# Two gate rows from matmuls of the spread products with ones, in a gMLP/S5 and PEER layer

## The chip, the core and the metric

The kernel runs on one core of a Trainium2 chip. The core has TensorE (PE, matmuls, with PEld for its weight loads), VectorE (DVE), ScalarE (ACT), GpSimd (POOL) and SyncE (SP, which issues transfers). The metric is the device time of one execution in microseconds (us), lower is better.

## The reference

One decoder layer on x of 1024 tokens x 1024, float32, with a conditioning vector c of 1024:

```python
mod = silu(c) @ w_ada + b_ada                      # 6 x 1024
sh1, sc1, gt1, sh2, sc2, gt2 = split(mod, 6)
h = rmsnorm(x, g_mix) * (1 + sc1) + sh1
z = h @ w_in                                       # u, v halves of a gMLP (512 each), S5 input (512)
y = concat(sgu(zu, zv), s5(zs)) @ w_out
x = x + gt1 * y
h2 = rmsnorm(x, g_ffn) * (1 + sc2) + sh2
x = x + gt2 * peer(h2)                             # 8 heads, product keys, top 16 of 16384 experts
return rmsnorm(x, g_final)
```

`gt1` and `gt2` are the gates: rows of 1024 numbers, the same for each token.

## The kernel before

The tokens are eight blocks of 128. The four blocks of a half share the input projection (`pzs` for the S5 input, `pzv` and `pzu` for the gMLP), and the S5 part is done for both halves at once: local convolutions and transfers of states as matmuls (`py` from `U`, `TOE` and from the scanned states `X` with `CN`), with the scan over chunks on VectorE in between (`t_s`, `X`, `fx`). The result `Yg` goes to DRAM (`ys_d`) and comes back transposed (`ysT`). Then come the GLU (`pg` matmuls with `wg`, sigmoid `sg`, product `ss`), the gMLP's mixing (`pmx`, `mx`, `gm`, from the normed `vn`), the output projection of a block (`po`, from `gm` and `ss` with `wo`), its gate and residual (`outproj`, L643 and L644: `po` times `bc`, plus `x`), the norm (`xn`), its transpose (`ptf`, `tq`), the PEER query (`pq`, with `wq`) and scores (`psc`, `sc`), and the routing on VectorE (`scr`, `m`, `ixs`). Blocks 0 to 4 go through a dense path: their gates are put into a table over all experts (`put`: `a`, `b`, `pgs`, `GS`), and from about 885 us on TensorE goes through 128 tiles of experts (`stage1`: `pa`; `stage2`: `res`, `pd`). Blocks 5 to 7 gather their experts' rows by indirect transfers on GpSimd beside that.

Each `mod[i]` is a column tile, 128 x 8. Its sums run on VectorE: eight chunks of `w_ada` (`wada`), each times its column of `cs` (the silu of c), are added into a spread tile of 128 x 1024 (`mp` in PSUM for i = 2 and 4, copied to `mc`; `mc` itself for i = 5, in `mod5`), so that what is left is the sum over the 128 partitions. `mod_late` does that sum with eight matmuls of 128x1 against a column of ones (`pm`) and adds the bias column. i = 2 is the first gate, i = 5 the second.

Where a gate is needed as a row over all partitions, `row_bcast` makes it from the column: for each of eight pieces VectorE writes a diagonal tile (`diag`), and a matmul of ones with it fills 128 columns of `pb`; ScalarE copies the 1024 columns to SBUF (`bc`). The first row (`gate1`, item `g1`) is used by all `outproj`. The second (`late_gt2`, item `gt`) is stored to DRAM (`gt2_d`) for the end of the kernel.

The tiles `mc`, `x`, `xn`, `mx`, `sg`, `bc2` share three slots (tag `x`); `mp`, `pb` and `po` share PSUM's tag `b`. Up to 885 us the code is written as generators, and an order of their steps is worked out from a table by hand (`plan`: start and duration of each item) and from each item's needs (`items`). A list scheduler then sets every engine's final order from that program and its own estimates; each engine takes its instructions strictly in that order.

Of the kernel before, what the change touches and what calls it, by code (L numbers as in the profile page):

```python
# [8 lines left out]
F32 = mybir.dt.float32  # L9
# [7 lines left out]
ALU = mybir.AluOpType  # L17
# [4 lines left out]
P = 128  # L22
S = 1024
D = 1024
KD = D // P
# [18 lines left out]
    op0=(-238.2, 44.5), sb0=(-21, 248.8), m5=(-490.1, 3.4), r0=(234.1, 82.1), op1=(132.1, 27.3), op2=(292.7, 7.7),  # L44
# [1 line left out]
    r2=(434.5, 89.3), s1=(746.9, 213.2), zu=(417.8, 124.5), sb3=(451.1, 27.3), r3=(536.2, 48.7),  # L46
    s2=(469.7, 305.5), gl=(553.5, 5.5), op4=(543.1, 6.2), op5=(577.6, 1.8), sb4=(663, 101), r4=(445.7, 88.9),
    s3=(833.5, 73.1), op6=(590.2, 7.7), sb5=(768.6, 1.7), op7=(897.9, 60.4), sb6=(809.8, 27.4), sb7=(892.4, 30.9),
    gt=(858.2, 122), rel=(739, 334), s4=(981.8, 131.5), r5=(916.4, 58.6), r6=(989.9, 124.6), ld=(776, 675.7),
    oa0=(-275.5, 62.3), oa1=(155.8, 9.5), oa2=(314.1, 7), oa3=(240.1, 5.1), oa4=(394.7, 40.1), oa5=(594, 15.7),  # L50
    oa6=(572.9, 5.5), oa7=(898.3, 28.1), z0=(-1650.9, 29.9), f1=(-1496.2, 24.1), z1=(-1253, 33.5),
    pa=(-1479.5, 58), pb=(-1364.9, 1.6), pc=(-1507.3, 44.1), cs=(-1171.2, 4.5), lu=(-1201.3, 17.4),
    k0=(-1496.6, 7.4), sn=(-1527.9, 6.3), m2=(-1355.9, 33), m4=(-1275.1, 28.3), pw=(-1348.9, 7.4),
    si=(-1231.9, 3.7), k1=(-1347, 1.5), av=(-1141.5, 2.5), wu=(-1185.4, 101), cst=(-1132.1, 14.6),
    sc=(-1112.1, 4.9), wq0=(-1115, 14.4), wq1=(-1142.8, 77.1), au=(-1181.6, 1.4), wo0=(-1165.4, 1),
    wo1=(-962.7, 7.3), so=(-926.7, 23.4), vn=(-891, 2.4), g1=(-703.9, 14.2), ax=(-882.1, 8.1), m3=(-856.1, 38.5),
    ag=(-741.7, 2.7), mid=(-803.3, 8.8), wo2=(-878.1, 13.4), wo3=(-805.6, 6.4), wq2=(-441.9, 1.1),
    wq3=(-808.5, 91.5), ky=(-851.1, 72.1)))

# [38 lines left out]
def tile_hybrid_layer(ctx: ExitStack, tc: tile.TileContext, a, out, cfg=CFG):  # L98
    nc = tc.nc
    V, A, G, T = nc.vector, nc.scalar, nc.gpsimd, nc.tensor  # L100
    NGB = cfg["ngb"]
    NDB = NB - NGB
# [23 lines left out]
    def bankB(name):  # L126
        return psB.tile([P, 2, 512], F32, tag="b", name=name)
# [81 lines left out]
    early = {}  # L209

    def mod_sums(i):
        mp = bankB(f"mp{i}").rearrange("p a b -> p (a b)")
        k = 0
        for w, n in early[i]:
            for kk in range(n):
                if k:
                    V.scalar_tensor_tensor(mp, w[:, kk], cs[:, k:k + 1], mp, op0=ALU.mult, op1=ALU.add)
                else:
                    V.tensor_scalar(mp, w[:, kk], cs[:, k:k + 1], None, op0=ALU.mult)
                k += 1  # L220
            yield
        mc = sm.tile([P, D], F32, tag="x", name=f"mc{i}", bufs=3)
        A.copy(mc, mp)
        mod_late(i, mc)

    def mod_load(i, src):
        ws, k = [], 0
        for c in src:
            n = {"X": 4, "p": 2, "x": 1}[c]
            v = a["w_ada"][k * P:(k + n) * P, i * D:(i + 1) * D].rearrange("(k p) n -> p k n", p=P)  # L230
            if c == "X":
                w = sB.tile([P, 4, D], F32, tag="X", name=f"wada{i}_{k}", bufs=1)
# [280 lines left out]
    wzu = []  # L513
# [16 lines left out]
    def z_u(hf, wz):  # L530
        y = slotA([P, 4, HT], f"gm{hf}")
        gm.append(y)
        for n in range(4):
            pz = bankA(f"pzu{hf}_{n}")
            for k in range(KD):
                T.matmul(pz, wz(k)[:, n * P:(n + 1) * P], hT[hf][k // 4][:, k % 4, :], start=(k == 0), stop=(k == KD - 1))
            A.activation(y[:, n, :], pz, AF.Gelu_apprx_tanh)
            yield
# [10 lines left out]
            if j % 2:  # L549
                yield  # L550

    def row_bcast(dst, col, name):
        pb = bankB(f"pb_{name}")
        for k in range(KD):
            dg = sm.tile([P, P], F32, tag="diag", name=f"diag_{name}{k}", bufs=2)
            V.tensor_scalar(dg, ident, col[:, k:k + 1], None, op0=ALU.mult)
            T.matmul(pb[:, k // 4, (k % 4) * P:(k % 4 + 1) * P], ones, dg, start=True, stop=True)
        A.copy(dst, pb.rearrange("p a b -> p (a b)"))
        return dst

# [36 lines left out]
    def load_wo(i, slot):  # L597
        wo[i] = slot([P, 2, D], f"wo{i}")
        nc.sync.dma_start(wo[i], a["w_out"][i * 256:(i + 1) * 256, :].rearrange("(k p) n -> p k n", p=P))

    def gate1():
        nonlocal gt1
        gt1 = row_bcast(sm.tile([P, D], F32, name="bc1", bufs=1), mod[2], "gt1")
        yield

    def glu(hf, slot):
        wg = slot([P, 4, 512], f"wg{hf}")
# [22 lines left out]
    def outproj(b):  # L630
# [19 lines left out]
                xns[b] = sm.tile([P, D], F32, tag="x", name=f"xn{b}", bufs=3)  # L650
                V.tensor_scalar(xns[b], x1, r2[:, b:b + 1], None, op0=ALU.mult)
        yield

    def late_gt2():
        bc2 = sm.tile([P, D], F32, tag="x", name="bc2", bufs=3)
        nc.scalar.dma_start(gt2_d, row_bcast(bc2, mod[5], "gt2"))

    gx = kp = sC = tk = iot = iot8 = None

# [386 lines left out]
    def lead(i0, i1):  # L1046
        for i in range(i0, i1):
            yield from stage1(i)

    def mod5():  # L1050
        mc = sm.tile([P, D], F32, tag="x", name="mc5", bufs=3)
        for k in range(0, KD, 2):
            w = slotC([P, 2, D], f"wada5_{k}")
            nc.sync.dma_start(w, a["w_ada"][k * P:(k + 2) * P, 5 * D:].rearrange("(k p) n -> p k n", p=P))
            for kk in range(2):
                if k + kk:
                    V.scalar_tensor_tensor(mc, w[:, kk], cs[:, k + kk:k + kk + 1], mc, op0=ALU.mult, op1=ALU.add)
                else:
                    V.tensor_scalar(mc, w[:, kk], cs[:, 0:1], None, op0=ALU.mult)
            if k == KD - 2:  # L1060
                mod_late(5, mc)
            yield

    def gt2_row():
        late_gt2()
        yield

    def mod4():
        yield from mod_sums(4)
# [2 lines left out]
    def prep_steps(n):  # L1072
# [10 lines left out]
        si=(s5_in, 4, "sn lu"), sc=(scan, 1, "si pw cs"), so=(s5_out, 8, "sc k1"),  # L1083
        av=(lambda: z_v(0, slotA([P, 4, 512], "vn0"), wzv), 4, "z0"), vn=(lambda: v_norm(0), 4, "av sc cst"),
        cst=(lambda: one(load_cst), 1, "z0"), wu=(lambda: one(load_wzu), 1, "z0"),
        au=(lambda: z_u(0, wzu[0]), 4, "wu"), ax=(lambda: mix(0), 2, "au vn"), g1=(gate1, 1, "m2"),
        ag=(lambda: glu(0, slotA), 4, "so"), mid=(mid, 1, "so m2 m4 m3"), m5=(mod5, 4, "mid sc"),
        ky=(lambda: one(lambda: nc.scalar.dma_start(keys, a["peer_keys"])), 1, "z0"),
        zv=(half1_v, 4, "mid vn z1"), zu=(half1_u, 6, "zv op1 op2 op3"), gl=(lambda: glu(1, slotS), 4, "ag"),
        gt=(gt2_row, 1, "m5"), rel=(release, NDB, "gt op7 sb7"), ld=(lambda: lead(0, L), 2 * L, "rel"))  # L1090
    for i in range(4):
        items[f"wq{i}"] = lambda i=i: one(load_wq, i), 1, f"wq{i - 1}" if i else "z0"
        items[f"wo{i}"] = lambda i=i: one(load_wo, i, slotC if i // 2 else slotS), 1, "mid" if i // 2 else "z0"
    for b in range(NB):
# [398 lines left out]
```

## Time and profile before

| | |
|---|---|
| runs | 2655.66, 2656.88, 2659.79 us; median 2656.88 |
| the profiled execution | 2655.86 us, span 2653.9 us |
| TensorE busy | 2538.1 us, 96% of the span |
| VectorE busy | 2267.8 us, 85% |
| ScalarE busy | 1312.8 us, 49% |
| GpSimd busy | 1180.9 us, 44% |
| transfers | 726.85 MB, 274 GB/s over the span |

A busy time is the time in which an engine executes; a busy engine isn't always the one that the end depends on. A matmul of float32 data leaves two records in the trace, so a "x16" of matmuls is eight instructions. The granted clock (PEclk) is 1.00 for 2.4 GHz and 0.50 for 1.2 GHz.

### The profile page before, as it was taken

To read this page: it belongs to the slowest core of one execution; us is meant where nothing else is said; L and a number is where in the kernel's file an instruction comes from. 1 tells how busy PE (TensorE), PEld (TensorE's weight loads), DVE (VectorE), ACT (ScalarE), POOL (GpSimd) and SP (SyncE) were. 2 spreads that over 40 slices of the span, in tenths; PEclk is the share of its full clock that TensorE was granted. 3 is DMA by queue.
4 is the path that set the end of the run, shared out by engine and by line. 5 is a ranking of instruction groups with operands and counts; after the bars stand their busy time and mean duration, and the time that the engine had idled before them with its cause. 6 is when DMAs were issued, how large, how long until landed. Compare 5 with 4: busy or idle time off the path is not lost. (4 is left out here: it accounts for less than half of the span.)

```text
span 2653.9 us, 39049 instructions
## 1 busy us (share of the span) xinstructions
PE 2538.1 (96%) x14119; PEld 2168.1 (82%) x14119; DVE 2267.8 (85%) x4215; ACT 1312.8 (49%) x2315; POOL 1180.9 (44%) x842
## 2 busy tenths in 40 slices
PE   6999999999877999999999999999999999999997
PEld 2548677678666898989999989999999988999986
DVE  7984699869899888789989888889999888899898
ACT  2311246568868377773222577762223767732222
POOL 0001000000000177676667578766665767776660
PEclk9996999999988999999999999999999999999999
DMA  9546233444636699999999999899998999999993
GB/s 362 108 121 217 101 122 104 126 136 135 181 118 193 218 328 326 343 327 364 341 340 375 325 336 330 331 354 364 341 355 326 334 345 343 325 368 345 343 365 139
DMA packets 301761, 726.85 MB, mean 274 GB/s; under 512 B 42448, under 2 KB 133072, under 8 KB 301152
## 3 DMA queue, kind: packets, MB, share of 16 engines
q0 software_dynamic: 112832, 411.09, 42.4%
q1 hardware_dynamic: 165600, 254.48, 28.6%
q10 hardware_dynamic: 23136, 58.79, 6.2%
q8 instruction: 111, 1.82, 0.3%
q14 instruction: 82, 0.67, 0.1%
HBM read 660.70 MB, written 62.39 MB: 272 GB/s over the span
## 5 line engine op out<-in xcount | busy, mean ns | idle before, releaser
L888 POOL DMA_INDIRECT ru<-in_peer_u_dram,ix x384 | 637.7, 1661 | 897.6 <-issue 745.1
L959 PE MATMUL pa<-Th,u 128*128 128x320 f32 x4096 | 911.3, 310 | 4.9 <-DVE u L936 3.1
L959 PEld LDWEIGHTS pa<-Th,u 128*128 128x128 f32 x4096 | 688.4, 188 | 8.7 <-DVE u L936 3.6
L888 POOL DMA_INDIRECT rv<-in_peer_v_dram,ix x384 | 522.8, 1361 | 257.4 <-DVE gacc L916 168.0
L959 PE MATMUL pa<-Tl,u 128*128 128x320 f32 x2048 | 633.4, 309 | 0.0
L899 DVE TENSOR_TENSOR ru<-ru,hn 128x2048 f32<-128x2048 f32 x192 | 438.6, 2289 | 113.1 <-DMA ru<-in_peer_u_dram,ix 106.6
L894 ACT ACTIVATE jk<-ru 128x1024 bf16<-128x1024 f32 x384 | 405.4, 1056 | 213.2 <-issue 167.7
L916 DVE SCALAR_TENSOR_TENSOR gacc<-rv,act,gacc 128x1024 f32<-128x1024 f32 x381 | 489.2, 1284 | 6.4 <-DVE u L936 0.4
L1006 PE MATMUL pd<-v,wh 128*128 128x512 f32 x1280 | 402.6, 390 | 3.2 <-ACT wh L980 1.6
L997 PE MATMUL res<-v,wh 128*128 128x512 f32 x1280 | 400.7, 390 | 0.8 <-ACT wh L980 0.8
L959 PEld LDWEIGHTS pa<-Tl,u 128*128 128x128 f32 x2048 | 385.3, 188 | 1.7
L1006 PEld LDWEIGHTS pd<-v,wh 128*128 128x128 f32 x1280 | 238.8, 188 | 52.5 <-ACT wh L980 2.5
L997 PEld LDWEIGHTS res<-v,wh 128*128 128x128 f32 x1280 | 239.6, 188 | 50.4 <-ACT wh L980 1.6
L961 ACT ACTIVATE w<-pa 128x320 f32<-128x320 f32 x256 | 108.7, 431 | 333.7 <-PE pa L959 311.9
L698 ACT ACTIVATE b<-hot,gT 128x128 f32<-128x128 f16 x520 | 233.5, 537 | 61.0 <-PE pgs L700 36.0
L1006 PE MATMUL pd<-v,wl 128*128 128x512 f32 x640 | 248.7, 390 | 1.7 <-DVE wl L982 1.6
L997 PE MATMUL res<-v,wl 128*128 128x512 f32 x640 | 248.1, 389 | 1.3 <-DVE wl L982 1.3
L935 ACT CAST u<-ur 128x1024 fp32r<-128x1024 f32 x128 | 133.5, 1043 | 205.3 <-DMA ur<-in_peer_ut_dram 79.0
L700 PE MATMUL pgs<-a,b 128*128 128x128 f32 x1280 | 188.9, 299 | 46.2 <-DVE a L690 19.3
L700 PEld LDWEIGHTS pgs<-a,b 128*128 128x128 f32 x1280 | 169.9, 207 | 68.4 <-ACT b L698 35.3
L936 DVE TENSOR_TENSOR u<-ur,u 128x1024 fp32r<-128x1024 f32 x128 | 156.3, 1221 | 29.7 <-ACT u L935 23.2
L943 ACT CAST v<-vr 128x1024 fp32r<-128x1024 f32 x128 | 133.7, 1045 | 94.1 <-DMA vr<-in_peer_v_dram 76.8
(349 smaller groups left out, 3050.4 us busy)
## 6 DMA issues: line engine op xcount, KB each, us to landing
vr<-in_peer_v_dram SPq DMA_DIRECT2D x128, 512.0 KB
ur<-in_peer_ut_dram SPq DMA_DIRECT2D x128, 512.0 KB
G_d<-GS SPq DMA_DIRECT2D x40, 1024.0 KB
Gt<-G_d ACTq DMA_DIRECT2D x64, 640.0 KB
wada<-in_w_ada_dram SPq DMA_DIRECT2D x17, 1024.0 KB
wo<-in_w_out_dram SPq DMA_DIRECT2D x8, 1024.0 KB
ru<-in_peer_u_dram,ix POOLq DMA_INDIRECT x384
rv<-in_peer_v_dram,ix POOLq DMA_INDIRECT x384
```

The lines of the kernel that those rows point to most:

```text
L698: A.activation(b1[:, n], hot[:, :, o + n], AF.Copy, scale=gT[:, s1 + o + n:s1 + o + n + 1])
L700: T.matmul(pg[:, o // 4, (o % 4) * P:(o % 4 + 1) * P], b1[:, o % 2], a1[:, o % 4], start=True, stop=True)
L888: G.indirect_dma_start(out=row[:, e], out_offset=None, in_=a[src], in_offset=bass.IndirectOffsetOnAxis(ap=ix[:, s0 + e:s0 + e + 1], axis=0))
L894: A.activation(junk, row[:, e], AF.Copy, accum_out=act[:, s + e:s + e + 1])
L899: V.tensor_mul(row, row, bcast(hn, 1, GP))
L916: V.scalar_tensor_tensor(ac, row[:, e], w, ac, op0=ALU.mult, op1=ALU.add)
L935: A.copy(u[:, 0], ur)
L936: V.tensor_tensor(u[:, 1], ur, u[:, 0].bitcast(F32), op=ALU.subtract)
L943: A.copy(v[:, 0], vr)
L959: T.matmul(pa[:, :NN], l[:, k, :], r[:, k, ns], start=(k == 0 and m == 0), stop=(k == KD - 1 and m == 2))
L997: T.matmul(res[tb][n], l[:, ts], r[:, n * 512:(n + 1) * 512], start=(g == 0 and q == 0 and m == 0), stop=(g == NGR - 1 and q == QG - 1 and ...
L1006: T.matmul(po, l[:, ts], r[:, n * 512:(n + 1) * 512], start=(q == 0 and m == 0), stop=(q == QG - 1 and m == 2))
```

## The change

`row_bcast` goes. A new function `gate_row` loads the gate's bias as one row (`br`, on one partition), and sums the spread products `mc` over the partitions with a whole matrix of ones as the stationary operand, so that each partition of `pb` gets the complete row; a second matmul over one partition adds the bias row. The first row is made at the end of `mod_sums(2)`, in place of `mod_late`; the second at the end of `mod5`, with its store. The items `g1` and `gt` go, and what needed them needs `m2` and `m5`.

```diff
@@ plan
-    gt=(858.2, 122), rel=(739, 334), s4=(981.8, 131.5), r5=(916.4, 58.6), r6=(989.9, 124.6), ld=(776, 675.7),
+    rel=(739, 334), s4=(981.8, 131.5), r5=(916.4, 58.6), r6=(989.9, 124.6), ld=(776, 675.7),
...
-    wo1=(-962.7, 7.3), so=(-926.7, 23.4), vn=(-891, 2.4), g1=(-703.9, 14.2), ax=(-882.1, 8.1), m3=(-856.1, 38.5),
+    wo1=(-962.7, 7.3), so=(-926.7, 23.4), vn=(-891, 2.4), ax=(-882.1, 8.1), m3=(-856.1, 38.5),
@@ mod_sums
         mc = sm.tile([P, D], F32, tag="x", name=f"mc{i}", bufs=3)
         A.copy(mc, mp)
-        mod_late(i, mc)
+        if i == 2:
+            gt1 = sm.tile([P, D], F32, name="bc1", bufs=1)
+            gate_row(i, mc, gt1)
+        else:
+            mod_late(i, mc)
@@ new
+    def gate_row(i, mc, dst):
+        br = sm.tile([P, D], F32, tag="x", name=f"br{i}", bufs=3)
+        nc.sync.dma_start(br[:1].rearrange("o (k p) -> o k p", p=P), a["b_ada"][:, i * KD:(i + 1) * KD].rearrange("p (o k) -> o k p", o=1))
+        pb = bankB(f"pb{i}")
+        for n in range(2):
+            for r, p in ((mc, P), (br, 1)):
+                T.matmul(pb[:, n], ones[:p], r[:p, n * 512:(n + 1) * 512], start=(p == P), stop=(p == 1))
+        A.copy(dst, pb.rearrange("p a b -> p (a b)"))
@@ gone
-    def row_bcast(dst, col, name):
-        pb = bankB(f"pb_{name}")
-        for k in range(KD):
-            dg = sm.tile([P, P], F32, tag="diag", name=f"diag_{name}{k}", bufs=2)
-            V.tensor_scalar(dg, ident, col[:, k:k + 1], None, op0=ALU.mult)
-            T.matmul(pb[:, k // 4, (k % 4) * P:(k % 4 + 1) * P], ones, dg, start=True, stop=True)
-        A.copy(dst, pb.rearrange("p a b -> p (a b)"))
-        return dst
...
-    def gate1():
-        nonlocal gt1
-        gt1 = row_bcast(sm.tile([P, D], F32, name="bc1", bufs=1), mod[2], "gt1")
-        yield
...
-    def late_gt2():
-        bc2 = sm.tile([P, D], F32, tag="x", name="bc2", bufs=3)
-        nc.scalar.dma_start(gt2_d, row_bcast(bc2, mod[5], "gt2"))
@@ mod5
             if k == KD - 2:
-                mod_late(5, mc)
-            yield
-
-    def gt2_row():
-        late_gt2()
-        yield
+                bc2 = sm.tile([P, D], F32, tag="x", name="bc2", bufs=3)
+                gate_row(5, mc, bc2)
+                nc.scalar.dma_start(gt2_d, bc2)
+            yield
```

In DRAM `b_ada` lies as 128 x 48, so that the 1024 numbers of a row `br` are 4-byte elements 192 bytes apart.

The program shows where the instructions now stand. On TensorE, between the last `pzv` (the v projection) and the first `py`, before:

```order
L491 MATMUL pzv_3_1100<-wzv_306,hT_1_130 128x512 x4
L248 MATMUL pm_1113<-ones,mc_1111 128x1 x8
L536 MATMUL pzu_0_1464<-hT_0_129,wzu_1123 128x512 x4
L536 MATMUL pzu_0_1464<-hT_1_130,wzu_1124 128x512 x4
L536 MATMUL pzu_1_1474<-hT_0_129,wzu_1123 128x512 x4
```

and of the change:

```order
L505 MATMUL pzv_3_1100<-wzv_305,hT_0_129 128x512 x4
L505 MATMUL pzv_3_1100<-wzv_306,hT_1_130 128x512 x4
L256 MATMUL pb_1116<-mc_1111,ones 128x512
L256 MATMUL pb_1116<-br_1114,ones 128x512
L256 MATMUL pb_1116<-mc_1111,ones 128x512
L256 MATMUL pb_1116<-br_1114,ones 128x512
L550 MATMUL pzu_0_1463<-hT_0_129,wzu_1122 128x512 x4
```

Eight matmuls of one column each have become four of 512 columns, ahead of the u projection (`pzu`) and all that follows. On TensorE between the last `pg` of the first half and the first `pq`, before (`pm_1900` is the column of row 5, `po_1916` and `po_2043` are blocks 0 and 1):

```order
L617 MATMUL pg_3_1848<-ysT_1818,wg_1816 128x512 x2
L637 MATMUL po_1916<-wo_1506,gm_1463 128x512
L557 MATMUL pb_gt_1857<-diag_gt_1873,ones 128x128
L557 MATMUL pb_gt_1857<-diag_gt_1876,ones 128x128
L637 MATMUL po_1916<-wo_1506,gm_1463 128x512
L637 MATMUL po_1916<-wo_1814,ss_1823 128x512 x4
L637 MATMUL po_1916<-wo_1812,ss_1823 128x512 x4
L557 MATMUL pb_gt_1857<-diag_gt_1879,ones 128x128
L637 MATMUL po_2043<-wo_809,gm_1463 128x512 x4
L637 MATMUL po_2043<-wo_1506,gm_1463 128x512 x4
L637 MATMUL po_2043<-wo_1814,ss_1823 128x512 x4
L637 MATMUL po_2043<-wo_1812,ss_1823 128x512
```

and of the change (`pb_1875`, `mc_1855` and `br_1873` are row 5's, `po_1888` and `po_2015` blocks 0 and 1):

```order
L617 MATMUL pg_3_1847<-ysT_1817,wg_1815 128x512
L256 MATMUL pb_1875<-mc_1855,ones 128x512
L256 MATMUL pb_1875<-br_1873,ones 128x512
L256 MATMUL pb_1875<-mc_1855,ones 128x512
L256 MATMUL pb_1875<-br_1873,ones 128x512
L637 MATMUL po_1888<-wo_809,gm_1462 128x512 x4
L637 MATMUL po_1888<-wo_1505,gm_1462 128x512 x4
L637 MATMUL po_1888<-wo_1813,ss_1822 128x512 x4
L637 MATMUL po_1888<-wo_1811,ss_1822 128x512 x4
L637 MATMUL po_2015<-wo_809,gm_1462 128x512 x4
L637 MATMUL po_2015<-wo_1505,gm_1462 128x512 x4
L722 MATMUL ptf_0_1927<-ident,xn_1924 128x128 x4
```

Row 5's matmuls now stand ahead of all of `po`, none of which is mixed with `pg` any more. On SyncE's queue, from the store of the first half of `Yg` on, the change has:

```order
L589 DMA ys_d<-Yg_1507 16x16x128 x4
L611 DMA ysT_1817<-ys_d 128x8x64
L597 DMA wq_1882<-in_w_q_dram 128x2x1024
L604 DMA wo_1811<-in_w_out_dram 128x2x1024
L604 DMA wo_1813<-in_w_out_dram 128x2x1024
L611 DMA ysT_1817<-ys_d 128x8x64
L1050 DMA wada_0_1856<-in_w_ada_dram 128x2x1024
L1050 DMA wada_2_1860<-in_w_ada_dram 128x2x1024
L597 DMA wq_1884<-in_w_q_dram 128x2x1024
L252 DMA br_1873<-in_b_ada_dram 1x1024x1
L1050 DMA wada_4_1864<-in_w_ada_dram 128x2x1024
L1050 DMA wada_6_1868<-in_w_ada_dram 128x2x1024
```

Before, `br` wasn't there and the second `ysT` stood ahead of the two `wo`.

## Rows read from the trace of the kernel before

**Rows 1.** Windows by stage: start:end, length, busy time of each engine, granted clock.

```profile
core 0: us, PE busy (x) PEld busy (x) DVE busy (x) ACT busy (x) POOL busy (x), PEclk, DMA share, GB/s
...
165.00:199.35 34.35, 31.86 (x99) 16.03 (x98) 33.42 (x81) 2.99 (x5) 1.37 (x4) 1.00 0.19 47
199.35:243.72 44.37, 44.37 (x190) 41.00 (x189) 20.98 (x48) 4.78 (x8) 1.43 (x2) 0.50 0.51 157
243.72:300.00 56.28, 55.18 (x221) 32.03 (x221) 28.76 (x54) 10.25 (x18) 7.28 (x50) 1.00 0.67 221
...
735.00:885.00 150.00, 110.51 (x703) 102.94 (x704) 137.96 (x621) 102.53 (x217) 0.00 (x0) 0.85 0.55 166
...
1300.00:2600.00 1300.00, 1298.49 (x7305) 1186.53 (x7304) 1143.81 (x947) 599.62 (x936) 884.32 (x595) 1.00 0.93 343
```

**Rows 2.** TensorE's timeline, 165 to 201: start, length, instruction, [idle before, who ended it].

```profile
165.21 1.84 PE L248 MATMUL pm<-ones,mc 128*128 128x1 f32 x16
166.91 27.71 PE L536 MATMUL pzu<-hT,wzu 128*128 128x512 f32 x64
194.46 1.05 PE L572 MATMUL py<-U,TOE 128*128 128x128 f32 x8
195.45 0.48 PE L578 MATMUL py<-X,CN 64*128 64x128 f32 x2
198.43 2.54 PE L578 MATMUL py<-X,CN 64*128 64x128 f32 x14 [2.49 <-DVE X L477]
```

**Rows 3.** VectorE's timeline, 175 to 283.

```profile
175.44 0.17 DVE L249 TENSOR_TENSOR mod<-pm,c_b_ada 128x8 f32<-128x8 f32 x1
...
175.89 0.47 DVE L556 TENSOR_SCALAR diag_gt<-ident,mod 128x128 f32<-128x128 f32 x2
176.28 0.38 DVE L448 TENSOR_TENSOR t_s<-A,X 128x128 f32<-128x128 f32 x1
...
218.70 2.49 DVE L510 TENSOR_TENSOR vn<-vn,cst 128x512 f32<-128x512 f32 x4
243.00 0.69 DVE L546 TENSOR_TENSOR mx<-pmx,cst 128x512 f32<-128x512 f32 x1 [21.81 <-PE pmx L544]
...
267.81 0.73 DVE L1059 TENSOR_SCALAR mc<-wada,cs 128x1024 f32<-128x1024 f32 x1
...
276.09 2.61 DVE L1057 SCALAR_TENSOR_TENSOR mc<-wada,cs,mc 128x1024 f32<-128x1024 f32 x2 [2.58 <-DMA wada<-in_w_ada_dram]
...
281.20 1.27 DVE L1057 SCALAR_TENSOR_TENSOR mc<-wada,cs,mc 128x1024 f32<-128x1024 f32 x1
```

**Rows 4.** SyncE's queue: the last store of zs and the loads that wait for it.

```profile
110.44 0.52 SPq L364 DMA_DIRECT2D zs_d<-zs  x1
116.82 1.78 SPq L374 DMA_DIRECT2D U<-zs_d  x4
```

**Rows 5.** TensorE's timeline, 240 to 309.

```profile
240.89 4.28 PE L544 MATMUL pmx<-cst,vn 128*128 128x128 f32 x24
...
251.79 4.46 PE L637 MATMUL po<-wo,gm 128*128 128x512 f32 x10
...
269.85 7.03 PE L637 MATMUL po<-wo,ss 128*128 128x512 f32 x16
...
278.20 7.13 PE L637 MATMUL po<-wo,gm 128*128 128x512 f32 x16 [1.10 <-ACT bc L558]
...
289.47 1.84 PE L248 MATMUL pm<-ones,mc 128*128 128x1 f32 x16
...
294.65 14.45 PE L736 MATMUL pq<-tq,wq 128*128 128x128 f32 x128
```

**Rows 6.** The gate rows by tile: ScalarE's copies (shortest, median, longest in ns).

```profile
L558 ACT COPY bc<-pb_gt x2: 1013/1022/1030, 277.1 to 753.6; 128x1024 f32<-128x1024 f32 x2
```

**Rows 7.** TensorE's timeline, 741 to 747.

```profile
741.04 1.25 PE L557 MATMUL pb_gt<-diag_gt,ones 128*128 128x128 f32 x4 [7.28 <-DVE diag_gt L556]
743.11 3.75 PE L700 MATMUL pgs<-a,b 128*128 128x128 f32 x16 [0.81 <-DVE x L644]
```

More of the change, by code (lines that the diff above doesn't have):

```diff
@@ L211, in mod_sums @@
     def mod_sums(i):
+        nonlocal gt1
         mp = bankB(f"mp{i}").rearrange("p a b -> p (a b)")
@@ L1085, in tile_hybrid_layer @@
         cst=(lambda: one(load_cst), 1, "z0"), wu=(lambda: one(load_wzu), 1, "z0"),
-        au=(lambda: z_u(0, wzu[0]), 4, "wu"), ax=(lambda: mix(0), 2, "au vn"), g1=(gate1, 1, "m2"),
+        au=(lambda: z_u(0, wzu[0]), 4, "wu"), ax=(lambda: mix(0), 2, "au vn"),
         ag=(lambda: glu(0, slotA), 4, "so"), mid=(mid, 1, "so m2 m4 m3"), m5=(mod5, 4, "mid sc"),
@@ L1089, in tile_hybrid_layer @@
         zv=(half1_v, 4, "mid vn z1"), zu=(half1_u, 6, "zv op1 op2 op3"), gl=(lambda: glu(1, slotS), 4, "ag"),
-        gt=(gt2_row, 1, "m5"), rel=(release, NDB, "gt op7 sb7"), ld=(lambda: lead(0, L), 2 * L, "rel"))
+        rel=(release, NDB, "m5 op7 sb7"), ld=(lambda: lead(0, L), 2 * L, "rel"))
     for i in range(4):
@@ L1096, in tile_hybrid_layer @@
         items[f"oa{b}"] = lambda b=b: outproj(b), 1, "zu" if h1 else "ax wo0 wo1"
-        items[f"op{b}"] = f"oa{b}", 1, f"oa{b} " + ("gl" if h1 else "g1 ag wo2 wo3")
+        items[f"op{b}"] = f"oa{b}", 1, f"oa{b} " + ("gl" if h1 else "m2 ag wo2 wo3")
         items[f"sb{b}"] = lambda b=b: score(b), NSC, f"op{b} wq3 ky m3 m4 mid"
```

## The prediction

> **What bounds the kernel now.** I read the windows by stage first. From 1300 to 2600 us TensorE is busy 1298.49 of 1300 us at full clock, and the stages after 885 us look much the same, so nothing that the change touches can be won there: its matmuls, products and copies all lie ahead of 885 us. What it can win or lose is the moment at which that full stretch begins. The stages before it show slack and one odd block: from 199.35 to 243.72 TensorE is busy all the time and the granted clock is 0.50, the lower of its levels, 1.2 GHz [rows 1]. Next I read TensorE's timeline around that block [rows 2], VectorE's and SyncE's between 175 and 288 us [rows 3, 4], TensorE's of the same stretch [rows 5], and last the gate rows themselves, by tile and on TensorE at 733 us [rows 6, 7].
>
> The reader should see three things. First, how the low block begins. TensorE ends the u projection (pzu), does ten records of py, and stands still for 2.49 us until the scan on VectorE hands over X at 198.43; 0.92 us later the clock is down [rows 1, 2]. It stays down through the whole of py, until pmx [rows 1, 5]. Second, py is work that everything behind it waits for: VectorE stands idle for 21.81 us until pmx, the first matmuls behind py, has given mx its input [rows 3]. Third, in 735 to 885 VectorE is busy 137.96 of 150 us and TensorE only 110.51 [rows 1].
>
> **The change, part by part.** *Row 2, the matmuls.* At 165.21 pm of the column (16 records, 1.70 us until pzu starts) gives way to four 128x512 matmuls. Sixteen records of the same shape take 7.03 us from 269.85 on [rows 2, 5], 0.44 each, and a matmul has two: 0.88 x 4 = 3.5 us. Two of the four contract over one partition, which no row shows. py's records on 64 partitions take 2.54/14 = 0.18 us each partly at the low clock, so a shallow matmul isn't free; the bounds are nothing (pb 1.76 us, no delay) and full price (3.5 us). I take full price, so pzu and the head of py come about 1.8 us later. The Trainium skill ("TensorE: Matmul & The Clock Gate", section "Why this matters for your kernels") says that a matmul with K=32 takes as long as one with K=128; by that rule the price is 3.5 us, and were it wrong, py would come no later and the gap below would hardly shrink.
>
> *Row 2, the scan.* On VectorE the add that made mod[2] (175.44, 0.17 us) and the two diagonal tiles at 175.89, 0.39 us together, stood in the middle of the scan [rows 3]. Allowing for some overlap the scan ends 0.3 us earlier. So the gap of 2.49 us shrinks to 2.49 - 1.8 - 0.3 = 0.4 us; with the one-partition matmuls free it would be 2.2.
>
> *What the clock makes of it.* In 243.72 to 300 there is a gap of 1.10 us (at 278.20), and that whole stretch has 1.00 [rows 1, 5]. So I take it that 0.4 us doesn't lower the clock and that py runs at 2.4 GHz. Then the 42.5 us from 198.43 to 240.89 become about 0.9 + 41.5/2 = 21.7 us; py ends near 219.9 instead of 240.9, 21 us earlier. vn, which pmx needs too, is done at 218.70 + 2.49 = 221.2 on VectorE [rows 3], so pmx begins there: 19.7 us earlier than at 240.89.
>
> *Row 5, where the 19.7 us go.* Before, TensorE took pg, po of block 0 and the pieces of pb_gt in turn, and started pq, the query of block 0, at 294.65 [rows 5]. Now, by the order above, pb of row 5 stands between pg and po, and TensorE takes its matmuls in order: po of block 0, po of block 1, ptf and pq are all queued behind the wait for mc5. mc5 is eight products. Before they went from 267.81 to 281.20 + 1.27, 14.7 us, with 2.58 us of wait for the third load, whose slot the first products had to free [rows 3]. They begin when the last sigmoid products (ss) are about done, which follow pg. 267.81 less the 19.7 us, and less about 6 more, since po (twelve records, 5.3 us) and pieces of pb_gt no longer lie between pg's matmuls, gives 242; the order sets one ysT transfer behind two 1 MB loads of w_out, which takes about a microsecond back. So mc5 is ready at 242 + 14.7 = 256 to 257. TensorE has nothing to do for some 15 us before, and I expect the lower clock when pb starts; pmx needed 2.83 us (240.89 to 243.72) to bring it back [rows 1, 5]. pb costs 3.5 us at full and 7 at half speed, po of block 0 takes 32 records x 0.44 = 14.1 us and 1.4 to 2.8 more until the clock is back. So po ends between 256 + 3.5 + 14.1 + 1.4 = 275 and 257 + 7 + 14.1 + 2.8 = 281; before it was 269.85 + 7.03 = 276.9. Behind it, po of block 1 (14.1 us), ptf and a first tq (some 2) give pq at 291 to 297. Near the middle of that I take 293.4, **1.3 us earlier** than 294.65: of the 19.7 us the wait for mc5 eats over 18. pm of row 5, 1.70 us at 289.47 ahead of ptf, falls away within this.
>
> *Cover.* The copies of the rows (1.02 us [rows 6]) are the same on ScalarE as before; the first now ends well before po needs it, and the wait of po of block 1 for that copy, 1.10 us, is gone [rows 5]. br of row 5 and mc5 take slots of tag x, and the load of x of block 0 now stands on ScalarE's queue behind the copy of row 5 and its store; that is near 265 us at worst, and the load then has 10 us until po is done. From 300 to 735 us the order is the same on every engine, so 1.3 us pass through.
>
> *The bias rows (br).* Each is a transfer of 1024 elements of 4 bytes on SyncE's queue. No row shows one like it; the nearest is zs_d, 1024 pieces of 256 bytes, from its issue at 110.44 (0.52 us) to 116.82, when the loads that wait for it go out: 6.4 us [rows 4]. Bounds: nothing, and 6.4 us. For row 2 it is issued among the TOE transfers, some 35 us ahead of 165; for row 5 ahead of the third and fourth load of w_ada, near 241, about 15 ahead of 256. It is hidden at either bound, unless SyncE waits at it for its slot and holds up those two loads. The Trainium skill ("DMA: Bandwidth & Descriptors", "Rules for kernel authors") says that a strided last dimension is lowered to one descriptor per element and advises against it; by that rule too the piece count is 1024, that of zs_d, and the trace bears out that such a store takes microseconds, not tens.
>
> *Row gt2, late.* Eight diagonals, eight matmuls, a copy and a store vanish between 733 and 754. On VectorE the diagonals cost 8 x 0.2 = 1.6 us, and VectorE is what that stage leans on. On TensorE the wait of 7.28 us goes, and with it some of the low clock after it, under which pgs took 3.75 us for 16 records [rows 7]. Bounds: 1.6 us (VectorE alone counts) and 1.6 + 7.3 = 8.9. The stage's engine is VectorE, and TensorE has 39.5 idle us in it, so I stay near the low end: **3.5 us**. The scheduler also moves xn, ptf and pq of block 7 behind some of pgs, which may give back or add some.
>
> *Sum.* -1.3 - 3.5 = -4.8. The profiled execution took 2655.86 us (1 us under the median of the runs): 2651 us, 0.22% under that median.
>
> **The rivals.**
> *The clock falls all the same* (slower). If the gap stays above what the chip bears, py runs at half speed as before, and pays for the wait on mc5 with nothing in return. It turns at a gap somewhere between 1.10 and 2.49 us [rows 2, 5]; the one-partition matmuls being cheap, or a later scan, would bring it there. Then pg starts as before, mc5 begins near 262 (no po in between) and ends at 277, pb and po, at a low clock first, end at 300, po of block 1 at 314 and pq starts at 316, 21 us later; less the 3.5 us late: about +14 to +19, 2670 to 2675.
> *Gain eaten.* mc5 comes at 257 and pb runs at half speed, so that pq starts at 296 or 297, or the late removal is worth only VectorE's 1.6 us. Then 2655 to 2662, no change that shows. For it speaks that the stage from 735 on has many other waits.
> *The late stage loses.* Block 7's xn and pq, moved back, hold up its scores and so the release; each of their steps (pq takes 128 records, 14.45 us [rows 5]) is longer than the gain. With 6 to 10 us lost: 2662 to 2666.
> *More comes through.* w_ada of row 5 finds its slots earlier and mc5 is ready near 251, or the late wait of 7.28 us goes in full: 5 us more, 2640 to 2646.
>
> **How the numbers follow.** A run of this kernel tells 0.2% (5.3 us) from no change. The forecast (2646 to 2655) has a chance of 0.47 and straddles that bound, half of it on either side; more coming through 0.16; gain eaten 0.13; the clock falling 0.15; the late stage losing 0.09. Faster is 0.235 + 0.16 = 0.4, the same 0.235 + 0.13 = 0.36, slower 0.15 + 0.09 = 0.24. The range 2641 to 2670 takes in all but the clock's fall and the far end of more coming through.
>
> **What would show it.** Granted clock 1.00 between 199 and 219 and a gap of under 1 us before py's X; pmx waiting for vn at 221; TensorE idle some 15 us with mc5 as what ends it, then pb at 0.5; pq of block 0 near 293; no wait for diagonals at 733. Wrong if the clock is at 0.50 from 199 on, if br ends any wait, or if pq of block 0 starts before 288.

## The result and the profile after

| | before | after |
|---|---|---|
| median (range) of 6 runs each | 2655.20 us (2650.76 to 2659.79) | 2672.76 us (2668.93 to 2674.12) |
| ratio after/before | | 1.0064 [1.0051, 1.0077] |
| the profiled execution (span) | 2655.86 (2653.9) | 2673.6 (2671.9) |
| TensorE / VectorE busy | 2538.1 / 2267.8 | 2531.7 / 2264.5 |

The kernel got 0.64% slower; 2651.0 was forecast, and 2641 to 2670 as the range. (A few executions of before and of experiments 5 and 6 take some 20 us less than their others, at a higher mean clock; medians and ratios count them.) No engine is busy longer than before (TensorE 6.4 us less), so the loss is waiting. The same stretches as in [rows 1], of the kernel after (start:end, length, busy time of PE, PEld, DVE, ACT, POOL, granted clock, DMA share, GB/s):

```profile
165.00:199.35 34.35, 34.35 (x88) 15.17 (x87) 33.32 (x80) 4.00 (x6) 1.69 (x4) 1.00 0.18 57
199.35:243.72 44.37, 36.51 (x249) 30.00 (x248) 25.99 (x57) 6.07 (x9) 8.66 (x52) 0.94 0.93 284
243.72:300.00 56.28, 39.67 (x71) 15.48 (x70) 17.80 (x27) 4.91 (x7) 0.00 (x0) 0.72 0.34 110
735.00:885.00 150.00, 110.87 (x652) 99.55 (x651) 129.35 (x587) 101.05 (x218) 0.00 (x0) 0.78 0.54 159
```

In the second stretch the clock rose from 0.50 to 0.94, and transfers from 157 to 284 GB/s. In the third the clock fell from 1.00 to 0.72, and TensorE's busy time by 15.5 us. TensorE's timeline after, which answers to [rows 2, 5]:

```profile
166.21 1.02 PE L256 MATMUL pb<-mc,ones 128*128 128x512 f32 x2
167.16 1.12 PE L256 MATMUL pb<-br,ones 1*128 1x512 f32 x2
...
170.32 27.73 PE L550 MATMUL pzu<-hT,wzu 128*128 128x512 f32 x64
197.89 1.05 PE L577 MATMUL py<-U,TOE 128*128 128x128 f32 x8
198.87 2.05 PE L583 MATMUL py<-X,CN 64*128 64x128 f32 x16
...
222.32 3.84 PE L558 MATMUL pmx<-cst,vn 128*128 128x128 f32 x32
...
227.70 7.11 PE L617 MATMUL pg<-ysT,wg 128*128 128x512 f32 x16
242.67 9.91 PE L617 MATMUL pg<-ysT,wg 128*128 128x512 f32 x16 [7.86 <-DMA ysT<-ys_d]
269.20 2.08 PE L256 MATMUL pb<-mc,ones 128*128 128x512 f32 x2 [16.61 <-DVE mc L1053]
271.20 2.07 PE L256 MATMUL pb<-br,ones 1*128 1x512 f32 x2
...
277.21 9.72 PE L637 MATMUL po<-wo,gm 128*128 128x512 f32 x16
286.76 7.03 PE L637 MATMUL po<-wo,ss 128*128 128x512 f32 x16
...
308.51 11.65 PE L732 MATMUL pq<-tq,wq 128*128 128x128 f32 x102
```

The gap of 2.49 us ahead of X is gone, py runs at full speed, and pmx starts 18.6 us earlier than before (222.32 for 240.89). Then come two waits. pg stands for 7.86 us until the second part of ysT has landed. At 252.58 pg is over, and TensorE stands for 16.61 us, until mc5 is made. Row 5's matmuls then take 2.0 us each, twice what the same shapes take at 166.21, and po's first sixteen records 9.72 us instead of 7.03. The query of block 0 starts at 308.51, 13.9 us later than before. VectorE after, which answers to the end of [rows 3]:

```profile
250.77 2.94 DVE L621 TENSOR_TENSOR ss<-ysT,sg 128x512 f32<-128x512 f32 x3 [22.11 <-ACT sg L620]
253.56 0.72 DVE L1055 TENSOR_SCALAR mc<-wada,cs 128x1024 f32<-128x1024 f32 x1
254.20 1.06 DVE L621 TENSOR_TENSOR ss<-ysT,sg 128x512 f32<-128x512 f32 x1
255.11 3.90 DVE L1053 SCALAR_TENSOR_TENSOR mc<-wada,cs,mc 128x1024 f32<-128x1024 f32 x3
263.89 5.25 DVE L1053 SCALAR_TENSOR_TENSOR mc<-wada,cs,mc 128x1024 f32<-128x1024 f32 x4 [4.89 <-DMA wada<-in_w_ada_dram]
```

The chain of mc5 lasts 15.6 us, from 253.56 to 269.14, much as before; it begins when the products ss are nearly through, and those follow pg and the sigmoid. SyncE's queue shows why ysT was late:

```profile
223.05 3.75 SPq L589 DMA_DIRECT2D ys_d<-Yg  x4
227.51 0.51 SPq L597 DMA_DIRECT2D wq<-in_w_q_dram  x1
228.25 1.95 SPq L604 DMA_DIRECT2D wo<-in_w_out_dram  x2
230.71 1.05 SPq L611 DMA_DIRECT2D ysT<-ys_d  x1
231.80 6.47 SPq L1050 DMA_DIRECT2D wada<-in_w_ada_dram  x2
238.31 0.47 SPq L597 DMA_DIRECT2D wq<-in_w_q_dram  x1
253.74 0.80 SPq L252 DMA_DIRECT2D br<-in_b_ada_dram  x1
256.39 3.01 SPq L1050 DMA_DIRECT2D wada<-in_w_ada_dram  x2
```

The load of ysT (256 KB) is issued at 230.71, behind one load of wq and two of wo, 1 MB each; TensorE gets it at 242.67, 12 us later. SyncE stood 15 us at br, until VectorE was done with the third ss (253.71), which by the times is when its tag x had a slot free. The two loads of w_ada behind it had to wait for the first products anyway (they end at 256.4), so that cost nothing.

Four marks divide the loss: pq of block 0, the first routing of block 5 on VectorE (scr), the first gather of block 5 on GpSimd (ru), and the span's end.

| mark, us | before | after | shift |
|---|---|---|---|
| first pq | 294.7 | 308.5 | +13.9 |
| first scr | 718.7 | 731.4 | +12.7 |
| first ru | 914.8 | 933.6 | +18.8 |
| end | 2653.9 | 2671.9 | +18.0 |

So 13.9 us are lost ahead of the first query, and about 5 more between pq and ru, all of it behind scr (6.1 lost there, 1.1 won ahead of it).

### The profile page after: what moved, and what is told of

It is laid out like the page before. It is cut to its first block, busy times and chain, and to the rows that moved or that the text cites. A ratio compares the mean times of both kernels' runs of the same rounds, so it can differ in the third digit from the quotient of the medians.

```text
span 2671.9 us, 38944 instructions
## 1 busy us (share of the span) xinstructions
PE 2531.7 (95%) x14071; PEld 2152.7 (81%) x14071; DVE 2264.5 (85%) x4197; ACT 1312.2 (49%) x2315; POOL 1176.8 (44%) x842
## 2 busy tenths in 40 slices
DMA packets 303824, 726.84 MB, mean 272 GB/s; under 512 B 44512, under 2 KB 135136, under 8 KB 303216
## 4 chain that ended last, share of the span: by engine, by line
PE 72%; DVE 14%; ACT 5%; DMA 4%; issue 2%; POOL 1%; ACTq 0%; DVEq 0%; POOLq 0%
PE pa L955 30%; PE res L993 15%; PE pd L1002 15%; ACT b L694 3%; PE pq L732 2%; PE po L637 2%; PE pzs L375 2%; PE pzu L550 2%; DVE a L686 1%; PE pgs L696 1%; DVE ixs L1376 1%; DVE ixs L1373 1%; PE pzv L505 1%; ACT GS L699 1%; DVE m L1372 1%
## 5 line engine op out<-in xcount | busy, mean ns | idle before, releaser
L884 POOL DMA_INDIRECT ru<-in_peer_u_dram,ix x384 | 630.4, 1642 | 937.3 <-issue 788.5
L940 DVE TENSOR_TENSOR v<-vr,v 128x1024 fp32r<-128x1024 f32 x128 | 156.2, 1220 | 20.0 <-ACT v L939 19.1
```

The source lines that it names most:

```text
L884: G.indirect_dma_start(out=row[:, e], out_offset=None, in_=a[src], in_offset=bass.IndirectOffsetOnAxis(ap=ix[:, s0 + e:s0 + e + 1], axis=0))
L940: V.tensor_tensor(v[:, 1], vr, v[:, 0].bitcast(F32), op=ALU.subtract)
```

## The experiments

The theory: the clock is won, and its gain lost again because row 5 stands ahead of po in TensorE's order. The rivals: the clock in py is worth little to the end; or the late removal loses by itself.

**1. Row 2 alone (e1_row2_only).** Row 5 by the column and the late diagonals, as before.

```diff
+    gt=(858.2, 122), rel=(739, 334), ...
...
-                gate_row(5, mc, bc2)
-                nc.scalar.dma_start(gt2_d, bc2)
+                mod_late(5, mc)
```

> Only the first gate row is made the new way; the second keeps its column, diagonals and late matmuls. If the loss comes from row 5's matmuls standing ahead of po (theory of the queue), nothing now holds po back: py at full clock ends near 221, pg still waits for ysT until about 242, pq of block 0 starts near 278 instead of 294.65 before, and the whole takes 2638 to 2645 us. If the loads behind py are the limit whatever the order (rival of the transfers), pq starts at 290 or later and the whole takes 2650 to 2656.

Measured: 2636.24 us (2629.93 to 2641.86, 12 runs), ratio 0.9933 [0.9906, 0.9959]; clock 1.00 from 199 to 244, pq at 280.2. This half gains 0.7%.

**2. Row 5 alone (e2_row5_only).** Row 2 by the column and diagonals, as before.

```diff
-                mod_late(5, mc)
+                gate_row(5, mc, bc2)
+                nc.scalar.dma_start(gt2_d, bc2)
```

> Only the second gate row is made the new way; the first keeps column and diagonals. py stays at half clock as before. Queue theory: po waits for mc5 with nothing gained before it, pq of block 0 starts at 312 to 318, the whole takes 2672 to 2682 us. Rival of the transfers: the wait for mc5 is short since the loads have 20 us more, pq at 300 or less, 2660 or less.

Measured: 2684.85 us (2681.71 to 2690.14, 6 runs), ratio 1.0119 [1.0079, 1.0159]. The gap and the low clock are there again (0.53 from 199 to 244), and so is the wait for mc5. TensorE's timeline of this run:

```profile
199.92 1.83 PE L587 MATMUL py<-X,CN 64*128 64x128 f32 x14 [2.49 <-DVE X L486]
...
281.82 2.07 PE L251 MATMUL pb<-mc,ones 128*128 128x512 f32 x2 [15.51 <-DVE mc L1062]
```

pq starts at 320.7. The loss is larger than the 2672 to 2682 us expected. So the wait isn't a product of the earlier pmx; row 5's place makes it, whenever pg ends.

**3. Row 5 later in the program (e3_m5_after_op1).** The table lets mod5 come behind block 1's output projection.

```diff
-    op0=(-238.2, 44.5), sb0=(-21, 248.8), m5=(-490.1, 3.4), ...
+    op0=(-238.2, 44.5), sb0=(-21, 248.8), m5=(165.0, 3.4), ...
```

> The changed kernel with one number of the plan changed: m5 starts behind op1 instead of ahead of oa0, so that row 5's loads, products and matmuls come behind po of blocks 0 and 1. Queue theory: pq of block 0 near 275 to 280, and the whole 2640 to 2648 us, some 25 to 33 under the changed kernel; the late stage alone (without the second row's diagonals) then shows its own effect as the difference to the run with row 2 only. Rival of the transfers: pq at 290 or later, 2655 or more.

Measured: 2653.58 us (2650.01 to 2661.64, 12 runs), ratio 1.0011 [0.9986, 1.0035], clock 1.00. The first wait moved behind pq:

```profile
273.38 16.19 PE L732 MATMUL pq<-tq,wq 128*128 128x128 f32 x128
291.34 1.10 PE L256 MATMUL pb<-mc,ones 128*128 128x512 f32 x2 [1.77 <-DVE mc L1053]
...
295.52 1.71 PE L743 MATMUL psc<-keys,tq 64*128 64x128 f32 x16
```

pq comes 35 us earlier than after, yet the whole gains only 19 by the medians (some 14 by the ratios), less than the 25 to 33 expected. psc, the scores, starts 22.1 us behind pq's start instead of the 14.4 of experiment 4, and the late part loses more than in the changed kernel (below).

**4. The kernel before with four idle matmuls (e4_before_filled).** Ahead of pzu; their results are not used. Nothing else changes.

```diff
         mod_late(i, mc)
+        if i == 2:
+            pf2 = bankB("fill2")
+            for n in range(4):
+                T.matmul(pf2[:, n % 2], ones, mc[:, n % 2 * 512:(n % 2 + 1) * 512], start=(n < 2), stop=(n > 1))
```

> The kernel before with four matmuls of 128x512 (their result isn't used) behind pm of row 2, so that TensorE comes 3.5 us later to the scan's wait and the gap of 2.49 us is gone. If the clock in py is what the shorter gap saves, the granted clock is 1.00 from 199 on, py ends near 221, pq of block 0 starts near 280 and the whole takes 2640 to 2646 us. If the clock falls in py for another reason, the time is 2656 to 2660.

Measured: 2635.27 us (2629.85 to 2641.89, 12 runs), ratio 0.9925 [0.9903, 0.9948]; pq at 278.1. Its stretch of py, to be held against [rows 1]:

```profile
199.35:243.72 44.37, 44.37 (x282) 34.97 (x281) 30.86 (x66) 6.66 (x10) 8.68 (x52) 1.00 0.87 257
```

More work on the busiest engine makes the kernel 20 us faster, as much as the whole of row 2. Within the noise the gain of row 2 is that of the clock, and the rival that it is worth little falls.

**5. The late row out (e5_late_row_out).** The kernel before without the second row: the first row is stored in its place, so the second gate's values are left out.

```diff
         gt1 = row_bcast(sm.tile([P, D], F32, name="bc1", bufs=1), mod[2], "gt1")
+        nc.scalar.dma_start(gt2_d, gt1)
...
-        gt=(gt2_row, 1, "m5"), rel=(release, NDB, "gt op7 sb7"), ...
+        rel=(release, NDB, "m5 op7 sb7"), ...
```

> The kernel before without the late second row: its diagonals, matmuls and copy between 733 and 754 are left out, and the first row is stored in its place (so the second gate's values are left out). Nothing changes ahead of 640 us but that store; behind, TensorE's order of block 7 is that of the changed kernel: ptf of block 7 behind 49 instead of 36 pgs. By the prediction's term the whole gains 1.6 to 9 us: 2646 to 2654. If the new order of the late stage costs, as the markers of the three runs with it say (their gathers start 5 to 10 us later than their scores would have them), it loses: 2660 to 2666.

Measured: 2663.61 us (2639.16 to 2668.23, 11 runs), ratio 1.0004 [0.9981, 1.0026]. The interval tells nothing from no change, since two of the runs had the high clock (0.982, at 2639 and 2640). The other nine have a median of 2663.9 against 2658.0 of before: 5.9 us slower with less work. From pq to ru the profile, of the slowest of the eleven, has 627.7 us against 620.1 of before.

**6. Row 2 without its bias (e6_row2_no_bias).** Experiment 1 without the load of br and the two matmuls over one partition; the first gate lacks its bias.

```diff
-            for r, p in ((mc, P), (br, 1)):
-                T.matmul(pb[:, n], ones[:p], r[:p, n * 512:(n + 1) * 512], start=(p == P), stop=(p == 1))
+            T.matmul(pb[:, n], ones, mc[:, n * 512:(n + 1) * 512], start=True, stop=True)
```

> The run with row 2 only, but without br and its two matmuls over one partition (the first gate's bias is left out): two matmuls instead of four, so that TensorE comes 2.1 us earlier to the scan's wait, with a gap near 1.8 us. If the gap decides (turning between 1.10 and 2.49 us), the time is either that of row 2 only (2630 to 2642) or some 20 us more, with the granted clock from 199 us on telling which; if it lies on the edge, single runs fall on both sides. If the one-partition matmuls were free, nothing would change in the gap: it would be under 0.5 us.

Measured: 2659.28 us (2638.44 to 2665.45, 12 runs), ratio 0.9994 [0.9971, 1.0017]. TensorE's timeline and the stretch of this run:

```profile
164.21 1.88 PE L253 MATMUL pb<-mc,ones 128*128 128x512 f32 x4
197.08 2.28 PE L589 MATMUL py<-X,CN 64*128 64x128 f32 x14 [2.23 <-DVE X L488]
```

```profile
199.35:243.72 44.37, 44.37 (x194) 41.23 (x194) 21.12 (x45) 4.78 (x8) 1.43 (x2) 0.51 0.54 153
```

Two matmuls of 1 us each over one partition decide over 23 us: without them the gap is 2.23 us and the clock falls, in nine of twelve runs (three lie at 2638 to 2641).

**7. TensorE kept at work during the wait (e7_after_kept_busy).** The changed kernel with fifteen matmuls ahead of row 5's, results not used.

```diff
+                fl = bankB("fill5")
+                for n in range(15):
+                    T.matmul(fl[:, n % 2], ones, ss[0][:, 3], start=(n < 2), stop=(n > 12))
                 gate_row(5, mc, bc2)
```

> The changed kernel with fifteen matmuls of 128x512 (their result isn't used) ahead of row 5's, which wait for ss and so fill most of the 16.6 us in which TensorE stood waiting for mc5. The wait stays; only the clock behind it is kept: pb of row 5 takes 4.2 instead of 8.0 us and po gains some 2.7. 2664 to 2668 if the clock is worth that, 2672 if not; pq of block 0 at 302 instead of 308.5.

Measured: 2671.01 us (2666.64 to 2679.41, 6 runs), ratio to before 1.0059 [1.0042, 1.0075]: no gain that can be told from the changed kernel's 1.0064.

```profile
254.43 13.14 PE L1060 MATMUL fill<-ss,ones 128*128 128x512 f32 x30 [2.73 <-DVE ss L621]
268.33 1.12 PE L256 MATMUL pb<-mc,ones 128*128 128x512 f32 x2 [0.76 <-DVE mc L1053]
269.39 1.12 PE L256 MATMUL pb<-br,ones 1*128 1x512 f32 x2
...
272.55 7.13 PE L637 MATMUL po<-wo,gm 128*128 128x512 f32 x16
...
301.27 14.56 PE L732 MATMUL pq<-tq,wq 128*128 128x128 f32 x128
```

pq comes 7.2 us earlier (308.51 to 301.27): 3.8 in pb and 2.6 in po are the clock after the wait, and mc5 was ready 0.9 earlier. In the profile, 5 of these were lost again from pq to ru (630.3 us for 625.1), but came back behind ru: its span is 2664.9 us for 2671.9. It is the fastest of the six runs, so how much of the 7.2 us reaches the end stays open.

**8. ysT on another queue (e8_after_ysT_act).** All four loads of a half on ScalarE's queue.

```diff
-            (nc.sync if k % 2 else nc.scalar).dma_start(ysT[:, k], ...)
+            nc.scalar.dma_start(ysT[:, k], ...)
```

> The changed kernel with all four loads of ysT on ScalarE's queue, so that none stands behind the two 1 MB loads of w_out on SyncE's. If the place in SyncE's queue makes pg wait (7.86 us at 242.67), pg ends some 7 us earlier, mc5 follows, and the whole takes 2664 to 2668. If the 16 shared transfer engines are simply full from 223 to 244, the loads come no earlier: 2670 to 2675.

Measured: 2678.99 us (2670.91 to 2682.36, 6 runs), ratio 1.0077 [1.0060, 1.0094], slower than the changed kernel. ysT went out at 232.24, on its own queue but now behind wq, two wo and two loads of w_ada on the other:

```profile
247.76 10.02 PE L617 MATMUL pg<-ysT,wg 128*128 128x512 f32 x16 [14.60 <-DMA ysT<-ys_d]
```

The place in SyncE's queue isn't what holds ysT. What fits is the amount issued before it, on any queue: the transfer engines are 93% busy in that stretch. Two other runs tell the price of the order. In experiment 4, as before, SyncE's second ysT goes out ahead of the two wo (234.08) and lands 6.7 us later; in experiment 1, as in the changed kernel, it goes out behind them (233.62) and lands 12.4 us later.

**9 and 10. Row 5's matmuls apart from its sum (e9_row5_late, e10_row5_mid).** Both rows by the new matmuls; the spread products mc5 are stored in `gt2_d` when made and loaded again where the row is made, at the old item's place (858.2 in the table), or at 700.

```diff
             if k == KD - 2:
-                bc2 = sm.tile([P, D], F32, tag="x", name="bc2", bufs=3)
-                gate_row(5, mc, bc2)
-                nc.scalar.dma_start(gt2_d, bc2)
+                nc.scalar.dma_start(gt2_d, mc)
             yield
+    def gt2_row():
+        mc = sm.tile([P, D], F32, tag="x", name="mc5b", bufs=3)
+        nc.scalar.dma_start(mc, gt2_d)
+        bc2 = sm.tile([P, D], F32, tag="x", name="bc2", bufs=3)
+        gate_row(5, mc, bc2)
+        nc.scalar.dma_start(gt2_d, bc2)
+        yield
```

> Both rows made the new way, but row 5's products are stored when they are ready and loaded again for a row that is made at the old late place (item gt at 858.2 as before), so that no matmul waits for mc5 ahead of po. Without row 5 in the queue and with the late order near that of before (ptf of block 7 behind 40 pgs): pq of block 0 near 277 and the whole 2630 to 2638 us, as the run with row 2 only or slightly less. If the diagonals' work in the late stage counted, it would be 3 us or more under that run; if the products' store and load cost, some us over it.

> The same but for one number of the plan: item gt at 700 instead of 858.2. The same work; row 5's matmuls then stand well ahead of the late stage, and its order is that of the changed kernel (ptf of block 7 behind 49 pgs). If that order is what costs 5 to 10 us in the changed kernel, this run is that much slower than the run with gt at 858.2 and the gathers start that much later after pq; if the absence of late work or the row's place were all, the two are equal within 3 us.

Measured: at the old place 2635.26 us (2634.59 to 2642.49, 6 runs), ratio 0.9925 [0.9913, 0.9938]; pq at 275.9, row 5's matmuls at 715.7. At 700: 2655.00 (2649.28 to 2659.71, 11 runs), ratio 0.9998 [0.9983, 1.0012]; pq at 279.9, the matmuls at 582.6. In the first, TensorE has po between pg's matmuls again, and the transfers' share of the stretch is 0.94 without any wait for them:

```profile
227.32 1.96 PE L617 MATMUL pg<-ysT,wg 128*128 128x512 f32 x4
229.12 1.02 PE L637 MATMUL po<-wo,gm 128*128 128x512 f32 x2
229.98 1.88 PE L617 MATMUL pg<-ysT,wg 128*128 128x512 f32 x4
...
242.85 3.60 PE L617 MATMUL pg<-ysT,wg 128*128 128x512 f32 x8
...
254.87 13.90 PE L637 MATMUL po<-wo,ss 128*128 128x512 f32 x32
275.87 16.40 PE L732 MATMUL pq<-tq,wq 128*128 128x128 f32 x128
```

pg's second half starts at 242.85, no earlier than in the changed kernel (242.67), but TensorE has done twenty records of po meanwhile. The same gate by the same matmuls, some 450 us later, turns +0.64% into -0.75%. This is the best version of the change; the idle matmuls of experiment 4 and row 2 alone do as well. The item at 700 instead costs 19.7 us, far more than the 5 to 10 expected, so the order of the late part alone doesn't explain it.

**11 to 14. Where the late part loses.** One number of the table in each run, to move block 7's scores, its norm and its projection against the other work.

```diff
e11, e12 (the latter on top of e3):  sb7=(892.4, 30.9) -> sb7=(892.4, 10.9)
e13:  r5=(916.4, 58.6) -> r5=(946.4, 58.6)
e14:  oa7=(898.3, 28.1) -> oa7=(850.3, 28.1)
```

> The changed kernel with one number of the plan changed: the duration of item sb7 (scores of block 7) from 30.9 to 10.9. The same work, and the same order on TensorE up to its row 909; behind, ptf of block 7 stands behind 40 pgs as with a late row, not 49. If the changed order of the late stage is what costs there, the gathers and stage 2 start 6 to 9 us earlier after the first routing of block 5 than in the changed kernel, and the whole takes 2663 to 2667 us; if the loss is elsewhere (no late row to fill TensorE's waits, or the clock), the time stays at 2671 to 2675.

> The run with m5 behind op1 with the same number changed (sb7's duration 10.9): the late order moved back in the same way behind another front. Late order costs: 2643 to 2648 us instead of 2653.6. Otherwise 2652 to 2656.

> The changed kernel with one number of the plan changed: item r5 (routing of block 5) from 916.4 to 946.4. The same work, and the same order on TensorE up to its row 887. On VectorE 62 instead of 145 instructions then stand between block 7's gated product and its xn. If xn's place on VectorE is what costs in the late stage, stage 2 starts 5 to 10 us earlier after pq of block 0 than in the changed kernel (there 597.5 us) and the whole takes 2662 to 2668 us; if it is the missing late work, nothing is gained: 2671 or more.

> The changed kernel with another number changed: item oa7 (output projection of block 7) from 898.3 to 850.3, the same order on TensorE up to its row 836. On VectorE 39 instructions stand between block 7's gated product and its xn. As for r5: 2662 to 2668 us if xn's place on VectorE is what costs, 2671 or more if not.

Measured: e11 2683.03 us (6 runs), ratio 1.0122 [1.0085, 1.0159]; e12 2659.40 (12), 1.0030 [1.0007, 1.0053]; e13 2682.88 (4), 1.0105 [1.0089, 1.0120]; e14 2670.82 (5), 1.0056 [1.0042, 1.0069]. None gives the loss back, and e11 and e13 lose some 10 us more, which was not expected of e11. That speaks against the place of block 7's ptf and pq on TensorE (e11, e12) as its cause, and against that of xn on VectorE (e13, e14); it doesn't exclude the latter, since scr came 17 to 20 us later in these two. The time from pq to ru, in the one profile of each:

| | pq to ru, us |
|---|---|
| second row at its old place: before, e4, e1, e9, e6 | 620.1, 619.8, 621.6, 621.0, 623.6 |
| no second row there: after, e8, e5, e2, e11, e14, e7, e13 | 625.1, 625.3, 627.7, 628.1, 628.1, 628.6, 630.3, 630.4 |
| second row made in between, earlier: e3, e10, e12 | 638.3, 638.7, 646.6 |

From scr to ru alone the first group takes 195.6 to 199.5 us, the second 202.1 to 206.6 (without e13 and e14, whose scr moved), the third 203.7 to 208.1. So the third loses behind scr what the second does; the rest of its loss lies ahead of scr, where its row now stands. From ru to the end the profiles take 1733 to 1743 us, in no order of these groups.

## Why the prediction was wrong, by its steps

**Right: row 2 and the clock.** pb was taken at full price, 3.5 us, and measured 4.1 (166.21 to 170.32): the two matmuls over one partition take 1.05 us each, no less than the others. The Trainium skill ("TensorE: Matmul & The Clock Gate", "Why this matters for your kernels") says that for K=32, and the trace bears it out at K=1. The gap of 0.4 us came out as none, py at 1.00, and pmx at 222.3, right behind py, where 221.2 was forecast. Experiments 4 and 6 show the step alone: with the gap filled by four idle matmuls the 20 us come, without the 2 us of the bias they don't in nine of twelve runs. The rival "the clock falls all the same" (0.15) did not happen; that the result lies in its bracket is chance.

**Wrong, first: "Row 5, where the 19.7 us go".** It has the right mechanism (po queued behind the wait for mc5), two terms too small and a third at its upper end. The chain of mc5 was to begin at 242 and began at 253.6. Of these 11.6 us, 7.9 are pg's wait for ysT, 2.8 pg's second half at a clock of 0.72 behind that wait (9.91 us for 7.11), and about 1 that pmx came later than forecast. The text gave the new order of the loads "about a microsecond": it saw ysT behind two loads of w_out, and priced the place in the queue and not the 3 MB in front at a transfer share of 0.93. Before, the second ysT went out ahead of wo; behind it, it lands 12.4 us after its issue instead of 6.7 (experiments 1 and 4), so the order's price is 5.7 us and not one. It took back nearly all of the "about 6" that po out of pg's matmuls was to win: in experiment 9, with po between them, pg's second half starts at the same time. Experiment 8 speaks for what is ahead on any queue: with 5 MB ahead the wait is 14.6 us. Second term: pb was 7 us at half clock and took 8.0. Third: po's recovery was 1.4 to 2.8, and took 2.7, its upper end. So mc5 came at 269.1 for 256.5, pq at 308.5 for 293.4, and the term -1.3 measured +13.9. Experiments 1, 9 and 4 bound it from the other side: without row 5 ahead of po, pq starts at 276 to 280 and the full gain reaches the end.

**Wrong, second: the late removal, -3.5.** It measured about +5 (pq to ru 625.1 for 620.1), and the same edit alone +5.9 in time and +7.6 from pq to ru (experiment 5). The step that failed is that a wait taken off TensorE was counted as a gain, and the new order ("may give back or add some") was put at nothing. The wait of 7.28 us for the diagonals did go [rows 7], but the changed kernel's TensorE waits at the same place for other things:

```profile
744.50 1.88 PE L637 MATMUL po<-wo,ss 128*128 128x512 f32 x4
746.22 2.27 PE L696 MATMUL pgs<-a,b 128*128 128x128 f32 x16
753.24 3.54 PE L696 MATMUL pgs<-a,b 128*128 128x128 f32 x16 [4.75 <-DVE a L686]
761.24 3.78 PE L696 MATMUL pgs<-a,b 128*128 128x128 f32 x16 [4.46 <-ACT b L694]
```

A wait taken out of TensorE came back under another name, on a and b, which fits a stretch that TensorE doesn't bound. The clock there fell from 0.85 to 0.78, but it is 0.78 in experiment 1 too, which has the row at its old place and doesn't lose from pq to ru. The rival "the late stage loses" (chance 0.09) thus happened in size, 5 to 8 of its 6 to 10 us. That a kernel without the row behind scr loses is shown by the times of experiment 5 and by the sixteen profiles, one of each kernel, whose groups don't overlap from pq to ru; its named mechanism, block 7's xn and pq, was only argued, and experiments 11 to 14 speak against it without excluding xn. Which of the moved or missing instructions costs it stays open.

**The sum.** -1.3 and -3.5 were forecast; +13.9 to pq and +5.0 from there to ru were measured, and 0.8 came back by the end: +18.0 in the span, 2673.6 for 2655.86 in the profiled executions.

**br** ended no wait of TensorE. Each of its two loads took 0.8 us to issue, and the transfers of the whole kernel count 2064 more packets under 512 B than before (44512 for 42448), about the 1024 per load that the prediction counted. SyncE did wait for br's slot, as the text allowed for; it had no price here.

## What to carry to other kernels

When a cheaper method merges two items into one, ask where its last instruction now stands in each engine's strict order: here four matmuls that save work held up the first blocks' projections until their operand was summed. Price a moved load by the bytes issued ahead of it, on all queues, while the transfer engines are full. And look at what happened just before a stretch at the low clock: filling a gap of 2.5 us with idle matmuls was worth as much as the whole of the useful half of this change.

## What the hardware showed that was not expected

- A float32 matmul of 512 columns over one partition took 1.05 us, as much as over 128 partitions (0.95, from 166.21 to 167.16), and 2.0 at the low clock.
- The same kernel has the clock of py lowered in most executions and, by the times, not in all. Of 95 runs of the kernel before in the experiments, nine lie at 2632 to 2645 us with a mean granted clock of 0.982 to 0.987, the others at 2648 to 2664 with 0.971 to 0.979. Where a profile shows the gap ahead of py (2.23 to 2.51 us: before and experiments 2, 5 and 6), the clock falls behind it; none of the nine was profiled, so whether they had the gap isn't shown. With the gap closed (experiments 1, 4 and 9) all 30 runs lie at 2630 to 2642.
- Once low, the clock stayed at 0.50 through 44 us in which TensorE was never idle [rows 1]: what ran was py, two thirds of its records over 64 partitions, and the clock rose 2.8 us after pmx had begun. In the changed kernel the same py, with no gap in it, ran at 1.00.
